# A token's gate matrix from a float32 product of 128 columns instead of a float32r product of 256

## The chip, the cores and the metric

The kernel runs on one core of a Trainium2 chip. The metric is the device time of one execution in microseconds (us), the median of several runs. In the rows, PE is TensorE (matrix products), PEld its loading of the stationary operand, DVE is VectorE, ACT is ScalarE, POOL is GpSimd and SP issues most loads.

## The reference, cut to what matters

One decoder layer over 512 tokens of width 2048: two token mixers, an output projection, a PEER channel mixer, a gated per-layer embedding and a last RMSNorm. The change lies in PEER. For each token, 8 heads choose 16 of 16384 experts each; an expert has the index `i1 * 128 + i2`, and a gate comes with it:

```python
e_idx = (jnp.take_along_axis(i1, ci // K, axis=-1) * PEER_NKEYS
         + jnp.take_along_axis(i2, ci % K, axis=-1))
gate = jax.nn.softmax(cv, axis=-1)
...
z = jnp.einsum('thkd,td->thk', u_tab[eb], hb)
a = jax.nn.gelu(z, approximate=False) * gb
return jnp.einsum('thk,thkd->td', a, v_tab[eb])
```

So a token has 128 pairs of an expert and a gate.

## The kernel before, in words

160 of the tokens go another way: their expert rows are gathered from memory by POOL, one row of every table access at a time, and DVE multiplies them (`row_op`, L915 and L924). The other 352 tokens are computed densely against all 16384 experts. The dense part has two stages. In the **u stage** a loop `j` over 128 tiles loads 128 experts' rows (1 MB), splits each float32 value into a high part (ACT, L115, written as float32r) and a low part (DVE, L116), and makes 48 products of 352 columns (L151, L152, L153). ACT applies the GELU (L1153). In the v stage the result, times the gates, is multiplied with the second table.

For that, each of the 352 tokens needs a matrix G of 128 by 128: the gate of expert (i1, i2) at row i1, column i2, and zero elsewhere. `gate_tokens` makes it during the u stage, four tokens at a time (a **quad** below; 88 in all). It compares a row of the numbers 0 to 127 (`iota`) with the token's 128 values of i1, which lie down the partitions, and so has a one-hot matrix `ohl` (two ACT operations, L997 and L1003). The same with i2, times the gate, is `ohr` (one DVE operation, L998). The product of the two (L1008) adds up 128 one-hot outer products into G. The products are float32r, a 4-byte format to which the code rounds; so the gate is held as a high and a low part, `ohr` has 2 times 128 columns, and the two halves of the result are added behind it, ACT copying the first (L1013) and DVE adding the second (L1014). `slots` holds i1, i2 and the two parts of the gate, transposed. A finished block of 32 tokens is stored by a transfer that ACT issues (L1016).

Three other lines come up below: L413 and L707 are float32 products of 128 by 128 (four for each of 8 heads in the first mixer, and the scores of the top-k), and L215 is a DVE operation of one scalar on a float32 matrix of 128 columns.

The order is written by hand. Each `j` takes steps of `gate_tokens` and of the top-k from a list by weights that the code states, and a fixed number of `row_op`; `gate_tokens` puts the quad's products behind that `j`'s 48 products, and its evacuation behind those of the next.

Of the kernel before, what the change touches and what calls it, by code (L numbers as in the profile page):

```python
# [10 lines left out]
F32 = mybir.dt.float32  # L11
F32R = mybir.dt.float32r
U32 = mybir.dt.uint32
I32 = mybir.dt.int32
AF = mybir.ActivationFunctionType
OP = mybir.AluOpType
# [34 lines left out]
def kernel(ctx: ExitStack, tc: tile.TileContext, a, dbg=None):  # L51
    nc = tc.nc
    dbg = dbg or {}
    V, S, G, TE = nc.vector, nc.scalar, nc.gpsimd, nc.tensor

    def flat(t):
        return t.rearrange("p a b -> p (a b)")
# [9 lines left out]
    def acc():  # L67
        return psA.tile([128, 512], F32, name="acc")
# [3 lines left out]
    def mx():  # L72
        return wide()[:, :512] if psW else psB.tile([128, 512], F32, name="mx")

    def wide():
        return psW.tile([128, 1024], F32, name="wide")

    def t2(name="t2", bufs=6):
        return tmp.tile([128, 512], F32, name="t2", bufs=bufs)
# [17 lines left out]
    class Stream:  # L97
# [14 lines left out]
        def split(self):  # L112
            for raw in self.raw:
                hi, lo = his(), los()
                S.activation(hi, raw, AF.Copy)  # L115
                V.tensor_tensor(lo, raw, hi.bitcast(F32), op=OP.subtract)  # L116
                self.parts.append((hi, lo))
# [46 lines left out]
    def cols_proj(src, xh, xl, kt=KT):  # L164

        w = Stream(src)
        ps = acc()
        for k in range(kt):
            mm3(ps, *w.part(k, kt), xh[:, k], xl[:, k], k == 0, k == kt - 1)
        return ps  # L170
# [74 lines left out]
    negmask, ident, iota = cst[:, :128], cst[:, 128:256], cst[:, 256:384]  # L245
# [5 lines left out]
    ones = const.tile([128, 128], F32, name="ones")  # L251
# [71 lines left out]
    for i in range(2):  # L323
        t = hg.tile([128, 4, 128], F32, name=f"abuf{i}")
# [10 lines left out]
    for hh in range(2):  # L335
# [25 lines left out]
        for c in range(4):  # L361
            ps = cols_proj(a["w_q"][hh * 4 + c], xh, xl)
            V.tensor_tensor(qT[:, c], ps, rr_mix, op=OP.mult)
        for c in range(4):
            ps = cols_proj(a["w_og"][hh * 4 + c], xh, xl)
# [24 lines left out]
        for h in range(4):  # L390
# [6 lines left out]
            for bb in range(2):  # L397
# [4 lines left out]
                o = slice(bb * 2, bb * 2 + 2)  # L402
# [15 lines left out]
            for n in range(7):  # L418
                dS = mx()
                r = slice((n % 2) * 64, (n % 2) * 64 + 64)  # L420
                TE.matmul(dS[:, :128], lhsT=k_t[r, n // 2, hs], rhs=v_t[r, n // 2, hs],
                          start=True, stop=True)
                st = hg.tile([128, 128], F32, name="st", bufs=8)
                if n == 0:
                    S.activation(st, dS[:, :128], AF.Copy)
                else:
                    V.scalar_tensor_tensor(st, states[-1], eb[:, n * 64 + 63:n * 64 + 64], dS[:, :128],
                                           op0=OP.mult, op1=OP.add)
                states.append(st)
            o_ps = mx()  # L430
            for b in range(4):
# [3 lines left out]
                for n in (2 * b, 2 * b + 1):  # L435
                    if n:
                        ns = slice(n * 64, n * 64 + 64)
                        TE.matmul(o_ps[:, ns], lhsT=states[n], rhs=qe[:, ns], start=False,
                                  stop=n == 2 * b + 1, skip_group_check=True)
# [28 lines left out]
    for name, src, gain in (("q", "w_mq", g_q), ("kv", "w_mkv", g_kv)):  # L468
# [3 lines left out]
        for c in range(4):  # L472
            ps = cols_proj(a[src][c], xh, xl)
            t = t2()
# [32 lines left out]
    ps = cols_proj(a["w_kr"][0], xh, xl)  # L507
    t = t2()
# [24 lines left out]
    for hp in range(4):  # L533
# [13 lines left out]
        for c in range(2):  # L547
            t = t2()
            V.tensor_tensor(t, lat_cols(c, qh, ql), rr_q, op=OP.mult)
            split(*qn[c], t)  # L550
        r, t = t2(), t2()
# [10 lines left out]
        for c in range(2):  # L562
            t = t2()
            V.tensor_tensor(t, lat_cols(c, vh, vl), rr_kv, op=OP.mult)
            split(*kn[c], t)
        for b, (bh, bl) in enumerate(vblocks):
            ps = acc()
            for k in range(4):
                hi, lo = w.part(k, 4)
# [6 lines left out]
        for c in range(2):  # L576
# [3 lines left out]
            for qb in range(4):  # L580
                n = (qb + 1) * 128
# [9 lines left out]
                st = tmp.tile([128, 4], F32, name="sm", bufs=4)  # L591
                V.tensor_reduce(st[:, 0:1], s_ps[:, :n], axis=AX.X, op=OP.max)
                V.tensor_scalar(st[:, 1:2], st[:, 0:1], -1.0, None, op0=OP.mult)
                p = t2()
# [9 lines left out]
                for kb in range(qb + 1):  # L604
                    TE.matmul(ob_ps[:, qs], lhsT=vv[:, kb, c * 128:c * 128 + 128],
                              rhs=pT[:, kb * 128:kb * 128 + 128], start=kb == 0, stop=kb == qb)
            t = t2()
# [135 lines left out]
    kpool = tc.alloc_tile_pool(name="kpool", bufs=1, side="left")  # L743
# [184 lines left out]
    def two(name, n=2):  # L928
        return (kpool.tile([128, 128], F32, name=name + str(i), bufs=2) for i in range(n))
# [13 lines left out]
    slots = {}  # L943
# [11 lines left out]
    def prep_B(b):  # L955
        i1, i2 = two("i")
        gt = kpool.tile([128, 128], F32, name="gt", bufs=1)

        def experts_X():
            e, x = t2()[:, :128], slice(0, NX)  # L960
            V.scalar_tensor_tensor(e[x], i1[x], 128.0, i2[x], op0=OP.mult, op1=OP.add)
            for r in range(RX):
                V.tensor_copy(eX[r * NX:(r + 1) * NX], e[x, r * NX:(r + 1) * NX])
                S.activation(gateX[r * NX:(r + 1) * NX], gt[x, r * NX:(r + 1) * NX], AF.Copy)

        def turn():
            slots[b] = kpool.tile([128, 4, 128], F32, name="slots", bufs=1)

            def pe():
                ps = mx()  # L970
                for n, t in enumerate((i1, i2, gt)):
                    TE.transpose(ps[:, n * 128:n * 128 + 128], t, ident)

                def act():
                    S.activation(flat(slots[b][:, :2]), ps[:, :256], AF.Copy)
                    split(slots[b][:, 2].bitcast(F32R), slots[b][:, 3], ps[:, 256:384])
                return act

            after_pe.append(lambda: after_pe_next.append(pe))
            hold[0] = 2  # L980

        return topk(b, i1, i2, gt) + ([(2, experts_X)] if b == 1 else []) + [(0, turn)]
# [3 lines left out]
    def gate_tokens(t0):  # L986

        if t0 % TC == 0:
            stage[0] = upool.tile([128, 128, TC], F32, name="stage", bufs=1)
        st = stage[0]  # L990
        hot = []
        for i in range(4):
            b, t = divmod(NA + NX + t0 + i, 128)
            l = upool.tile([128, 128], F32R, name="ohl", bufs=8)
            r = upool.tile([128, 2, 128], F32R, name="ohr", bufs=8)
            i1T, i2T = (slots[b][:, n, t:t + 1] for n in range(2))
            S.activation(l, iota, AF.Abs, scale=-1.0, bias=i1T)  # L997
            V.scalar_tensor_tensor(r, iota[:, None, :].to_broadcast([128, 2, 128]), i2T,  # L998
                                   slots[b][:, 2:4, t:t + 1].to_broadcast([128, 2, 128]),
                                   op0=OP.is_equal, op1=OP.mult)  # L1000
            hot.append((l, r))
        for l, _ in hot:
            S.activation(l, l.bitcast(F32), AF.Relu, scale=-1.0, bias=ones[:, :1])  # L1003

        def pe():
            ps = wide()
            for i, (l, r) in enumerate(hot):
                TE.matmul(ps[:, i * 256:i * 256 + 256], lhsT=l, rhs=flat(r), start=True, stop=True)  # L1008

            def act():  # L1010
                o = t0 % TC
                hi, lo = (ps.rearrange("p (t s j) -> p s j t", t=4, s=2)[:, n] for n in range(2))
                S.activation(st[:, :, o:o + 4], hi, AF.Copy)  # L1013
                V.tensor_tensor(st[:, :, o:o + 4], st[:, :, o:o + 4], lo, op=OP.add)  # L1014
                if o == TC - 4:
                    nc.scalar.dma_start(G_s[t0 // TC], flat(st))  # L1016
            return act

        after_pe.append(pe)
        if t0 % TC == TC - 4:  # L1020
            hold[0] = 2

    def merge(*lists):
# [3 lines left out]

    first = NA + NX
    quads = {b: [(2, lambda t=t - first: gate_tokens(t)) for t in range(max(b * 128, first), (b + 1) * 128, 4)]
             for b in (1, 2, 3)}  # L1030

# [33 lines left out]
    for n, (src, dst) in enumerate((("w_ga", ga_s[1]), ("w_gb", gb_s[1]))):  # L1065
        for i in range(16):
            w = block(a[src][i])
            ps = acc()[:, :H]
# [29 lines left out]
    for k in range(2):  # L1098
        r = t2()
# [4 lines left out]
    for m in range(16):  # L1104
# [5 lines left out]
        t = t2()  # L1110
# [30 lines left out]
    upool = tc.alloc_tile_pool(name="upool", bufs=1, side="left")  # L1141
# [37 lines left out]
    in_u, start = ops[0] - VROWS, ops[0]  # L1179
    for j in range(NU):  # L1180
# [5 lines left out]
        n = j + 1  # L1186
# [52 lines left out]
    def v_products(cur, grp, half):  # L1239
        ps = acc()[:, :ND]  # L1240
        for j in range(NJ):
            mm3(ps, *cur.part(half * NJ + j, 2 * NJ), *aT[grp, j], j == 0, j == NJ - 1)
        return ps

    NV = (NGRP - 1) * 8
    for grp in range(NGRP - 1):
        for dp in range(8):
            n = grp * 8 + dp
# [11 lines left out]
            for half in range(2):  # L1260
                ps = v_products(cur, grp, half)
# [33 lines left out]
    for dp in range(8):  # L1295
        cur = ahead.step()
        run_late()
        ps = [v_products(cur, NGRP - 1, half) for half in range(2)]
# [30 lines left out]
    for mt in range(16):  # L1329
# [8 lines left out]
        ps = acc()  # L1338
# [179 lines left out]
```

## Time and profile before

| | |
|---|---|
| median of three runs | 3962.06 us (3954.68 to 3966.48) |
| the profiled execution | 3957.45 us |
| its span in the trace | 3955.7 us |
| mean granted clock of TensorE in it | 0.993 of full |

The profiled execution's own time is its span and 1.75 us around it. The quads lie between 1754 us and 2676 us of that span.

### The profile page before, as it was taken

What the parts mean: (1) busy time and instruction counts of PE and PEld (TensorE: products, weight loads), DVE (VectorE), ACT (ScalarE), POOL (GpSimd) and SP (SyncE); (2) the same over time, 40 slices, a digit from 0 to 9 for tenths busy, and PEclk for the clock granted to TensorE, in tenths of its full rate; (3) what the DMA queues carried; (4) which work ended last, traced back from release to release, by engine and by line L of the source; (5) the groups of instructions that cost most, each with busy time, mean ns of one, the idle gap of its engine ahead of it and who ended that gap; (6) DMA issues with size and microseconds to landing.
All of it is one profiled execution on the core that took longest, in us unless ns stands there. A gap on an engine that the chain in (4) does not pass through costs nothing. (4 is left out here: it accounts for less than half of the span.)

```text
span 3955.7 us, 63576 instructions
## 1 busy us (share of the span) xinstructions
PE 3873.2 (98%) x24825; PEld 3677.9 (93%) x24825; DVE 2950.8 (75%) x4439; ACT 1750.3 (44%) x2814; POOL 496.4 (13%) x326
## 2 busy tenths in 40 slices
PE   9999999999999999899999999999999999999998
PEld 7878788899999989899999999999999999999987
DVE  5252555557658798789989898886888989899854
ACT  5242434345544434455555466663333333333443
POOL 0000000000000111012222222221122222222000
PEclk9999999999999999999999999999999999999999
DMA  5222234457766988788888888989999999899533
GB/s 212 96 75 96 70 99 134 130 184 238 231 203 205 330 280 299 268 293 314 317 319 301 306 324 308 338 310 357 359 346 346 368 356 353 330 360 361 195 120 99
DMA packets 312875, 1011.64 MB, mean 256 GB/s; under 512 B 29952, under 2 KB 127744, under 8 KB 269696
## 3 DMA queue, kind: packets, MB, share of 16 engines
q1 hardware_dynamic: 224032, 595.02, 44.1%
q0 software_dynamic: 46080, 335.56, 22.3%
q10 hardware_dynamic: 42464, 77.00, 5.1%
q8 instruction: 196, 3.21, 0.3%
q14 instruction: 103, 0.84, 0.1%
HBM read 931.18 MB, written 76.28 MB: 255 GB/s over the span
## 5 line engine op out<-in xcount | busy, mean ns | idle before, releaser
L116 DVE TENSOR_TENSOR lo<-raw,hi 128x1024 fp32r<-128x1024 f32 x966 | 1163.7, 1221 | 599.2 <-ACT hi L115 590.7
L115 ACT ACTIVATE hi<-raw 128x1024 fp32r<-128x1024 f32 x966 | 1012.5, 1056 | 1222.1 <-PE acc L152 819.1
L153 PE MATMUL acc<-hBh,lo 128*128 128x352 f32 x2048 | 662.1, 323 | 0.0
L152 PE MATMUL acc<-hBl,hi 128*128 128x352 f32 x2048 | 661.0, 323 | 0.0
L151 PE MATMUL acc<-hBh,hi 128*128 128x352 f32 x2048 | 658.7, 322 | 0.0
L904 POOL DMA_INDIRECT row<-in_peer_u_dram,eA x128 | 206.5, 1613 | 2194.2 <-PE acc L153 1298.8
L153 PEld LDWEIGHTS acc<-hBh,lo 128*128 128x128 f32 x2048 | 385.5, 188 | 0.0
L151 PEld LDWEIGHTS acc<-hBh,hi 128*128 128x128 f32 x2048 | 385.3, 188 | 0.0
L152 PEld LDWEIGHTS acc<-hBl,hi 128*128 128x128 f32 x2048 | 384.9, 188 | 0.0
L153 PE MATMUL acc<-ahx,lo 128*128 128x352 f32 x1024 | 331.5, 324 | 2.0 <-DVE lo L116 1.9
L151 PE MATMUL acc<-ahx,hi 128*128 128x352 f32 x1024 | 329.9, 322 | 1.1 <-DVE x L1237 1.1
L153 PE MATMUL acc<-ah,lo 128*128 128x352 f32 x1024 | 330.4, 323 | 0.5 <-DVE lo L116 0.5
L151 PE MATMUL acc<-ah,hi 128*128 128x352 f32 x1024 | 330.9, 323 | 0.0
L152 PE MATMUL acc<-alx,hi 128*128 128x352 f32 x1024 | 330.4, 323 | 0.0
L152 PE MATMUL acc<-al,hi 128*128 128x352 f32 x1024 | 329.0, 321 | 0.0
L151 PE MATMUL acc<-xh,hi 128*128 128x256 f32 (+1 forms) x912 | 305.1, 335 | 0.0
L153 PE MATMUL acc<-xh,lo 128*128 128x256 f32 (+1 forms) x912 | 305.0, 334 | 0.0
L152 PE MATMUL acc<-xl,hi 128*128 128x256 f32 (+1 forms) x912 | 304.2, 334 | 0.0
L924 DVE SCALAR_TENSOR_TENSOR hrow<-row,zA,hrow 128x2048 f32<-128x2048 f32 x127 | 297.9, 2345 | 0.8
L915 DVE SCALAR_TENSOR_TENSOR row<-row,hrow 128x2048 f32<-128x2048 f32 x128 | 291.6, 2281 | 6.8 <-DMA row<-in_peer_u_dram,eA 6.8
L904 POOL DMA_INDIRECT row<-in_peer_v_dram,eA x128 | 188.2, 1470 | 645.3 <-DVE hrow L924 610.5
L153 PEld LDWEIGHTS acc<-ahx,lo 128*128 128x128 f32 x1024 | 192.6, 188 | 3.7 <-DVE lo L116 3.7
(434 smaller groups left out, 8430.7 us busy)
## 6 DMA issues: line engine op xcount, KB each, us to landing
raw<-in_uT_dram SPq DMA_DIRECT2D x256, 512.0 KB, 7.5
raw<-in_vB_dram SPq DMA_DIRECT2D x256, 512.0 KB, 8.4
raw<-in_w_ga_dram SPq DMA_DIRECT2D x64, 512.0 KB, 4.2
raw<-in_w_gb_dram SPq DMA_DIRECT2D x64, 512.0 KB, 4.7
raw<-in_w_o_dram SPq DMA_DIRECT2D x64, 512.0 KB, 4.9
raw<-in_wq_dram SPq DMA_DIRECT2D x64, 512.0 KB, 4.7
z_s<-t ACTq DMA_DIRECT2D x128, 176.0 KB, 6.7
G_s<-stage ACTq DMA_DIRECT2D x11, 2048.0 KB, 15.0
```

What stands on the lines that cost most here:

```text
L115: S.activation(hi, raw, AF.Copy)
L116: V.tensor_tensor(lo, raw, hi.bitcast(F32), op=OP.subtract)
L151: TE.matmul(out, lhsT=lh, rhs=rh, start=start, stop=False)
L152: TE.matmul(out, lhsT=lh, rhs=rl, start=False, stop=False)
L153: TE.matmul(out, lhsT=ll, rhs=rh, start=False, stop=stop)
L904: G.indirect_dma_start(out=row, out_offset=None, in_=a["peer_v" if v else "peer_u"], in_offset=bass.IndirectOffsetOnAxis(ap=e[:, s:s + 1], ...
L915: V.scalar_tensor_tensor(row, row, 1.0, hrowX if x else hrow, op0=OP.mult, op1=OP.mult, accum_out=(zX if x else zA)[:, s:s + 1])
L924: V.scalar_tensor_tensor(o, row, c[:, s:s + 1], o, op0=OP.mult, op1=OP.add)
```

## The change: what it does

The quad's products become float32 products of 128 columns: `ohl` and `ohr` are float32, `ohr` holds the whole gate in one 128 by 128 matrix, and the result needs no addition, so ACT's copy alone takes it into `stage`. `slots` holds three transposed blocks instead of four, and one ACT copy fills it.

```diff
@@ turn, in prep_B @@
-            slots[b] = kpool.tile([128, 4, 128], F32, name="slots", bufs=1)
+            slots[b] = kpool.tile([128, 3, 128], F32, name="slots", bufs=1)
...
-                    S.activation(flat(slots[b][:, :2]), ps[:, :256], AF.Copy)
-                    split(slots[b][:, 2].bitcast(F32R), slots[b][:, 3], ps[:, 256:384])
+                    S.activation(flat(slots[b]), ps[:, :384], AF.Copy)
@@ gate_tokens @@
-            l = upool.tile([128, 128], F32R, name="ohl", bufs=8)
-            r = upool.tile([128, 2, 128], F32R, name="ohr", bufs=8)
-            i1T, i2T = (slots[b][:, n, t:t + 1] for n in range(2))
+            l = upool.tile([128, 128], F32, name="ohl", bufs=8)
+            r = upool.tile([128, 128], F32, name="ohr", bufs=8)
+            i1T, i2T, gT = (slots[b][:, n, t:t + 1] for n in range(3))
             S.activation(l, iota, AF.Abs, scale=-1.0, bias=i1T)
-            V.scalar_tensor_tensor(r, iota[:, None, :].to_broadcast([128, 2, 128]), i2T,
-                                   slots[b][:, 2:4, t:t + 1].to_broadcast([128, 2, 128]),
-                                   op0=OP.is_equal, op1=OP.mult)
+            V.tensor_scalar(r, iota, i2T, gT, op0=OP.is_equal, op1=OP.mult)
...
-            S.activation(l, l.bitcast(F32), AF.Relu, scale=-1.0, bias=ones[:, :1])
+            S.activation(l, l, AF.Relu, scale=-1.0, bias=ones[:, :1])
...
-            ps = wide()
+            ps = mx()
             for i, (l, r) in enumerate(hot):
-                TE.matmul(ps[:, i * 256:i * 256 + 256], lhsT=l, rhs=flat(r), start=True, stop=True)
+                TE.matmul(ps[:, i * 128:i * 128 + 128], lhsT=l, rhs=r, start=True, stop=True)
...
-                hi, lo = (ps.rearrange("p (t s j) -> p s j t", t=4, s=2)[:, n] for n in range(2))
-                S.activation(st[:, :, o:o + 4], hi, AF.Copy)
-                V.tensor_tensor(st[:, :, o:o + 4], st[:, :, o:o + 4], lo, op=OP.add)
+                S.activation(st[:, :, o:o + 4], ps.rearrange("p (t j) -> p j t", t=4), AF.Copy)
```

The order of the instructions stays: on every engine each remaining instruction stands between the same neighbours as before, and rows are replaced or left out. On PE, at the first two quads of the u stage, the products of a whole `j` stand ahead (`hBh`, `hBl`, `hi` and `lo` are the operands of L151 to L153); before:

```order
L152 MATMUL acc<-hBl,hi_77 128x352
L153 MATMUL acc<-hBh,lo_81 128x352
L1008 MATMUL wide<-ohr,ohl 128x256 x8
L151 MATMUL acc<-hBh,hi_78 128x352
L152 MATMUL acc<-hBl,hi_78 128x352
```

and with the change:

```order
L152 MATMUL acc<-hBl,hi_77 128x352
L153 MATMUL acc<-hBh,lo_81 128x352
L1005 MATMUL wide<-ohr,ohl 128x128 x8
L151 MATMUL acc<-hBh,hi_78 128x352
L152 MATMUL acc<-hBl,hi_78 128x352
```

The quad's products keep their place; the line is now L1005. On DVE, from the same two quads on (`row` and `zA` are `row_op`'s, `scores` and `val` the top-k's), before:

```order
L998 SCALAR_TENSOR_TENSOR ohr<-cst,slots 128x256 x8
L915 SCALAR_TENSOR_TENSOR row_6472,zA<-row_6472,hrow 128x2048
L116 TENSOR_TENSOR lo_80<-raw_72,hi_76 128x1024
L116 TENSOR_TENSOR lo_81<-raw_73,hi_77 128x1024
L1014 TENSOR_TENSOR stage<-stage,wide 128x128x4 x2
L830 MAX val<-scores 128x8 x2
```

and with the change:

```order
L997 TENSOR_SCALAR ohr<-cst,slots 128x128 x8
L915 SCALAR_TENSOR_TENSOR row_6472,zA<-row_6472,hrow 128x2048
L116 TENSOR_TENSOR lo_80<-raw_72,hi_76 128x1024
L116 TENSOR_TENSOR lo_81<-raw_73,hi_77 128x1024
L830 MAX val<-scores 128x8 x2
```

The addition is gone and the one-hot operation is another one of half the columns; nothing else on DVE changes its place.

## Rows read from the trace of the kernel before

**Rows 1.** The page's first part: each engine's busy time over the span.

```profile
PE 3873.2 (98%) x24825; PEld 3677.9 (93%) x24825; DVE 2950.8 (75%) x4439; ACT 1750.3 (44%) x2814; POOL 496.4 (13%) x326
```

**Rows 2.** Windows of the u stage: the stretch, its length, busy us of each engine.

```profile
1734.00:2690.00 956.00, 951.39 (x5990) 946.22 (x5989) 855.76 (x1391) 552.04 (x1159) 217.16 (x126) 1.00 0.87 316
...
2500.00:2600.00 100.00, 100.00 (x640) 100.00 (x640) 87.62 (x115) 65.88 (x147) 23.82 (x14) 1.00 0.89 323
```

**Rows 3.** The quads' products, line L1008: counts, durations, idle time before them.

```profile
L1008 PEld LDWEIGHTS wide<-ohr,ohl x352: 186/188/288, 1756.9 to 2672.3; 128*128 128x128 f32 x176
L1008 PE MATMUL wide<-ohr,ohl x352: 274/281/554, 1757.1 to 2672.4; 128*128 128x256 f32 x176
its engine sat idle before it (us, times) until:
  issue: 4.3, 17
  DVE ohr L998: 3.1, 3
  ACT t L1153: 2.8, 2
  ACT ohl L1003: 2.1, 3
  ACT hi L115: 0.2, 1
  ACT stage L1013: 0.2, 1
```

**Rows 4.** Timeline of PE at the first two quads: start us, length us.

```profile
1757.05 1.10 PE L1008 MATMUL wide<-ohr,ohl 128*128 128x256 f32 x8
1757.99 0.32 PE L151 MATMUL acc<-hBh,hi 128*128 128x352 f32 x1
1758.15 0.32 PE L152 MATMUL acc<-hBl,hi 128*128 128x352 f32 x1
```

**Rows 5.** Timeline of PE at two float32 products of 128 columns, L707.

```profile
1733.39 0.33 PE L153 MATMUL acc<-hBh,lo 128*128 128x352 f32 x1
1733.56 0.61 PE L707 MATMUL mx<-kk_t,t 128*128 128x128 f32 x4
1733.92 0.41 PE L151 MATMUL acc<-hBh,hi 128*128 128x352 f32 x1
1734.16 0.32 PE L152 MATMUL acc<-hBl,hi 128*128 128x352 f32 x1
```

**Rows 6.** Timelines of PE at four float32 products in a row, L413, twice.

```profile
200.47 1.05 PE L413 MATMUL mx<-e,e 128*128 128x128 f32 x8
201.45 0.71 PE L421 MATMUL mx<-v_t,k_t 64*128 64x128 f32 x6
...
227.60 1.16 PE L413 MATMUL mx<-e,e 128*128 128x128 f32 x8
228.69 0.71 PE L421 MATMUL mx<-v_t,k_t 64*128 64x128 f32 x6
```

**Rows 7.** Line L413 over the whole span: counts, durations ns.

```profile
L413 PEld LDWEIGHTS mx<-e,e x64: 186/192/193, 200.3 to 449.1; 128*128 128x128 f32 x64
L413 PE MATMUL mx<-e,e x64: 270/275/374, 200.5 to 449.2; 128*128 128x128 f32 x64
```

**Rows 8.** Timeline of DVE and PE around the latest quads.

```profile
2068.71 3.26 DVE L998 SCALAR_TENSOR_TENSOR ohr<-cst,slots 128x256 fp32r<-128x256 f32 x8
2076.37 1.27 DVE L1014 TENSOR_TENSOR stage<-stage,wide 128x512 f32<-128x512 f32 x2
2079.92 1.66 DVE L998 SCALAR_TENSOR_TENSOR ohr<-cst,slots 128x256 fp32r<-128x256 f32 x4
2084.45 1.74 PE L1008 MATMUL wide<-ohr,ohl 128*128 128x256 f32 x4 [2.38 <-DVE ohr L998]
```

**Rows 9.** Timeline of DVE at four float32 TENSOR_SCALAR of 128 columns, L215.

```profile
3772.73 0.87 DVE L215 TENSOR_SCALAR t<-cst,rc_ple 128x128 f32<-128x128 f32 x4
```

## The prediction

> **What bounds the kernel now.** I read the page's busy shares first [rows 1]: PE is busy for 3873.2 of 3955.7 us, and the next engine, DVE, for 75%. A share over the whole span says little about one stage, so the windows of the u stage come next, in which all 88 quads lie [rows 2]. From 1734 to 2690 us PE is busy for 951.4 of 956.0 us, DVE for 855.8. PE waits for almost nothing there, and where no quad is late (2500 to 2600 us, 13 quads) for nothing at all. So whatever is put on PE in this stage comes out at the end, and what is taken from DVE or ACT counts only as far as PE waits for it.
>
> Then the changed line itself [rows 3]. It has one record for each of its 352 products, and the idle times ahead of it add up to 4.3 + 3.1 + 2.8 + 2.1 + 0.2 + 0.2 = 12.7 us. That is an upper bound on what less work on DVE and ACT can give back here; some of it counts one wait twice, for the load and for the product behind it, and the idle time of PE in rows 2 is only 4.6 us.
>
> Last, the price of a product. A record's duration (281 ns at the median) is no price, since products overlap. The price is the distance from one start to the next, so I read timelines.
>
> **What PE pays.** Before: eight products of two quads start at 1757.05, and the next L151 at 1757.99 [rows 4]. That is 0.94 us, 0.1175 us for a product, 0.47 us for a quad, and 352 x 0.1175 = 41.4 us in all.
>
> After: the trace has no float32 product with these operands, but float32 products of 128 rows by 128 columns elsewhere. The nearest are the two of L707 that stand, as the quads will, between products of 352 columns [rows 5]. They leave four records, two for each product. From their start at 1733.56 to the second product behind them, at 1734.16, it is 0.60 us; one product of 352 columns takes 0.16 us of it (from L151 to L152 in rows 4). The L151 between is drawn early and long, so its own start is no good mark. That leaves 0.44 us for two, 0.22 us for one, 0.88 us for a quad. In all 352 x 0.22 = 77.4 us.
>
> The difference is 77.4 - 41.4 = **+36.0 us**, 0.41 us for a quad.
>
> The other rows give the bounds. L413 has four float32 products in a row, each with its own stationary operand, as a quad has. Eight records take 0.98 us to the next start, and 1.09 us in another place [rows 6]: 0.245 and 0.273 us a product, +44.8 and +54.7 us in all. No row is below 0.22 us. I take 0.22, because rows 5 has the quads' neighbours, while in rows 6 the next product has 64 rows and may itself start late, and because a quad's operands are ready long before its turn but for the waits counted below.
>
> A rule of the Trainium skill speaks against this change. Its page "TensorE: Matmul & The Clock Gate", section "Weight-path perf modes", says that the fast way to load the stationary operand is not used for FP32. The rows show no slower load: 192 ns at the median for L413's float32 operand [rows 7], 188 ns for float32r [rows 3]. What loads that could not be hidden would do is a rival below.
>
> **What the waits give back.** On DVE the four `ohr` operations of a quad halve their columns and become TENSOR_SCALAR. Eight of before take 3.26 us, 0.41 each [rows 8]; four float32 TENSOR_SCALAR of 128 columns take 0.87 us, 0.22 each [rows 9]. Those have one scalar operand from a column and the new one has two, as the old one has; I take 0.22, with 0.41 as the other end. The addition L1014 goes, 1.27 / 2 = 0.64 us. Together 4 x 0.19 + 0.64 = 1.4 us for a quad, 123 us of DVE. None of it is on PE's path except where PE waits for `ohr`.
>
> The largest such wait is 2.38 us at 2084.45 [rows 8]. Ahead of it DVE does twelve `ohr` operations and two additions from 2068.71 on, with other work between; with the change that is 12 x 0.19 + 1.27 = 3.6 us less, more than the wait. So waits of this kind go. What stays is what ACT ends: its two operations for `ohl` keep their number and size, and PE waits 2.1 us for them [rows 3]. I take **-10 us** of the 12.7; the ends are 0 and -12.7.
>
> **The rest at nothing.** One ACT copy instead of the three operations for `slots` happens three times in the run, beside PE's 48 x 0.16 = 7.7 us of products in a `j`. ACT's copy into `stage` has the same 512 columns. The result's buffer holds 512 columns instead of 1024 but comes from the same two, in the same turn. No transfer, no gather and no `row_op` moves, since their number in each `j` is fixed, so the v stage begins later by what the u stage takes longer, and no queue is passed. If the new `ohr` cost as much as the old, those 7.7 us would still hide it as they do now, and only the waits would not go: +36.
>
> **Sum.** 36.0 - 10 = +26.0 us on an execution of 3957.45 us (span 3955.7 and 1.75 around it): 3983.5 us. The median of the runs shown is 3962.06, 4.6 us above that execution, so in such a median I expect **3988 us**.
>
> **Rivals.**
>
> *The second pass starts late in each quad.* The 1.09 us of rows 6 would be the rule, not the exception: 54.7 - 10 = +44.7, 4007 us. For it speaks that PE comes to a quad with other operands than those of its 48 products; against it rows 5, with the same neighbours. Chance 0.14. I count in it the case that the waits stay (+36 to +45).
>
> *Loads bind.* Eight loads of 192 ns [rows 7], if they did not lie beside the passes, take 1.54 us a quad instead of 0.47: +94, less 10, 4046 us. Against it: rows 6 has eight records with eight loads in 0.98 us. Chance 0.03. The Trainium skill's page "FP8 and Floating Point Precision", section "TensorE Precision Notes", gives a true FP32 product four passes through the array. The rows show two records a product, so by the rule each record would stand for two passes; four passes at a record's 0.11 us would be +113 us, and rows 5 and 6 exclude that.
>
> *One pass (the other side).* If the new product went through once, as the old does, half the columns would take half the time: 0.059 us, 0.235 us a quad, -20.7 us, and with the waits -31 us, 3931 us. It decides where a quad costs less than 0.47 + 10 / 88 = 0.58 us. Against it: 64 records for L413's 32 products [rows 7] (four for each of 8 heads), and four for two in rows 5. Chance 0.03.
>
> *It cancels.* Two passes of 0.059 us, half a record's 0.11 us, would be 0.1175 us a product, as before, and only the waits would count: -10 us, 3952 us, which is within 0.3%. Against it rows 5 again. Chance 0.05, with all else that ends near zero, such as waits outside rows 3 that go with DVE's 123 us.
>
> That the change would not do what it says I leave at nothing: the built order has the new rows in the old places.
>
> **How the numbers follow.** Forecast 0.75, late second pass 0.14, loads 0.03, one pass 0.03, cancels 0.05. A measurement of this kernel can tell about 0.3% (12 us) from no change, so slower is 0.75 + 0.14 + 0.03 = 0.92, same 0.05, faster 0.03. The range's low end is the forecast with all 12.7 us back, 3985, less 6 us for half the spread of the three runs: 3979. Its high end is the price of rows 6 with no wait gone, +45, 4007, and with it the first rival's 4007: I take 4008.
>
> **What would show it.** In the changed kernel's profile L1005 should have 704 product records and 704 loads, and two quads should keep PE for about 1.76 us to the next L151 or L152 instead of 0.94; a quad at 1.0 or more is the first rival, and 352 records the third. DVE's busy time over the u stage should fall by about 120 us, and PE should still be busy for over 99% of it. The idle times ahead of the quads' products should add up to 3 us or so. The u stage should end some 26 us later, and every stage outside it should take what it takes now. The prediction is wrong if a float32 pass costs something else between these neighbours than between L707's, or if PE waits for DVE somewhere that I have not seen.

## The result: 26 us slower

The changed kernel takes 3986.5 us in the median of five runs (3985.12 to 3995.72), beside 3960.49 us (3954.68 to 3966.48) for five runs of the kernel before. The ratio of the mean times is 1.0072, with a 95% interval from 1.0055 to 1.0088, that is 22 to 35 us. The forecast was 3988 us, 26 us more. That the two medians differ by just these 26.0 us is luck: such runs can't tell it so closely.

The page of the changed kernel, first part, answers to [rows 1]:

```profile
PE 3904.4 (98%) x25177; PEld 3713.3 (93%) x25177; DVE 2851.5 (72%) x4348; ACT 1754.5 (44%) x2811; POOL 465.4 (12%) x326
```

PE has 25177 products instead of 24825, so 352 more, one for each token. DVE does 99 us less work. The stage in which the quads lie, by the first and the last start of L151's products in the u stage (its row by line, before and then the changed kernel):

```profile
L151 PE MATMUL acc<-hBh,hi x2048: 317/323/496, 1725.8 to 2764.2; 128*128 128x352 f32 x187
```

```profile
L151 PE MATMUL acc<-hBh,hi x2048: 318/324/408, 1727.5 to 2791.6; 128*128 128x352 f32 x187
```

The stage takes 1038.4 us before and 1064.1 after: 25.7 us more. The two profiled executions differ by 28.7 us of span (3984.4 and 3955.7 us), and the other 3.0 us lie ahead of the u stage (1.7 us) and behind it. Below, "the u stage" is this length, read in the same way from each run's trace.

The windows of the u stage, drawn 26 us longer, and the changed line, answer to [rows 2] and [rows 3]:

```profile
1734.00:2716.00 982.00, 980.95 (x6345) 980.75 (x6344) 756.74 (x1303) 555.35 (x1156) 187.26 (x127) 1.00 0.85 309
```

```profile
L1005 PEld LDWEIGHTS wide<-ohr,ohl x704: 186/192/192, 1758.6 to 2699.7; 128*128 128x128 f32 x176
L1005 PE MATMUL wide<-ohr,ohl x704: 270/275/348, 1758.8 to 2699.8; 128*128 128x128 f32 x176
...
its engine sat idle before it (us, times) until:
  ACT hi L115: 1.2, 1
  DVE ohr L997: 1.1, 1
```

Each product has two records and two loads. PE is busy for 99.9% of the stage, and the idle times ahead of the quads are 2.3 us instead of 12.7 (here one wait of 1.1 us, counted for the load and again for the product). The first two quads in the timeline of PE, which answer to [rows 4]:

```profile
1758.79 1.95 PE L1005 MATMUL wide<-ohr,ohl 128*128 128x128 f32 x16
1760.49 0.41 PE L151 MATMUL acc<-hBh,hi 128*128 128x352 f32 x1
1760.74 0.32 PE L152 MATMUL acc<-hBl,hi 128*128 128x352 f32 x1
```

From 1758.79 to the second product behind, 1760.74, less 0.16 us for one product of 352 columns, is 1.79 us for eight products: 0.224 us each. In the whole trace 75 of the 76 places where quads stand (12 of them hold two) cost 0.112 us a record in this way; in the other one PE waits for `ohr`.

### The profile page after: what moved, and what is told of

Its sections match the earlier page's. It is cut to its first block, busy times and chain, and to the rows that moved or that the text cites. A ratio compares the mean times of both kernels' runs of the same rounds, so it can differ in the third digit from the quotient of the medians.

```text
span 3984.4 us, 64143 instructions
## 1 busy us (share of the span) xinstructions
PE 3904.4 (98%) x25177; PEld 3713.3 (93%) x25177; DVE 2851.5 (72%) x4348; ACT 1754.5 (44%) x2811; POOL 465.4 (12%) x326
## 3 DMA queue, kind: packets, MB, share of 16 engines
q8 instruction: 199, 3.26, 0.3%
## 5 line engine op out<-in xcount | busy, mean ns | idle before, releaser
L151 PE MATMUL acc<-hBh,hi 128*128 128x352 f32 x2048 | 664.3, 324 | 0.0
L153 PE MATMUL acc<-hBh,lo 128*128 128x352 f32 x2048 | 661.3, 323 | 0.0
L152 PE MATMUL acc<-hBl,hi 128*128 128x352 f32 x2048 | 660.5, 323 | 0.0
L904 POOL DMA_INDIRECT row<-in_peer_u_dram,eA x128 | 196.7, 1537 | 2217.2 <-PE acc L153 1299.2
L151 PEld LDWEIGHTS acc<-hBh,hi 128*128 128x128 f32 x2048 | 384.9, 188 | 0.0
L153 PEld LDWEIGHTS acc<-hBh,lo 128*128 128x128 f32 x2048 | 384.9, 188 | 0.0
L152 PEld LDWEIGHTS acc<-hBl,hi 128*128 128x128 f32 x2048 | 384.8, 188 | 0.0
L153 PE MATMUL acc<-ahx,lo 128*128 128x352 f32 x1024 | 331.3, 324 | 2.8 <-DVE lo L116 2.7
L151 PE MATMUL acc<-ahx,hi 128*128 128x352 f32 x1024 | 329.7, 322 | 2.1 <-DVE x L1232 2.1
L151 PE MATMUL acc<-ah,hi 128*128 128x352 f32 x1024 | 330.5, 323 | 0.2 <-DVE x L1232 0.2
L152 PE MATMUL acc<-alx,hi 128*128 128x352 f32 x1024 | 330.3, 323 | 0.0
L153 PE MATMUL acc<-ah,lo 128*128 128x352 f32 x1024 | 329.6, 322 | 0.5 <-DVE lo L116 0.5
L152 PE MATMUL acc<-al,hi 128*128 128x352 f32 x1024 | 328.6, 321 | 0.0
L151 PE MATMUL acc<-xh,hi 128*128 128x256 f32 (+1 forms) x912 | 304.9, 334 | 0.0
L153 PE MATMUL acc<-xh,lo 128*128 128x256 f32 (+1 forms) x912 | 304.8, 334 | 0.0
L152 PE MATMUL acc<-xl,hi 128*128 128x256 f32 (+1 forms) x912 | 304.0, 333 | 0.0
L153 PEld LDWEIGHTS acc<-ahx,lo 128*128 128x128 f32 x1024 | 192.5, 188 | 4.8 <-DVE lo L116 4.8
```

The lines of the kernel that those rows point to most:

```text
L151: TE.matmul(out, lhsT=lh, rhs=rh, start=start, stop=False)
L152: TE.matmul(out, lhsT=lh, rhs=rl, start=False, stop=False)
L153: TE.matmul(out, lhsT=ll, rhs=rh, start=False, stop=stop)
L904: G.indirect_dma_start(out=row, out_offset=None, in_=a["peer_v" if v else "peer_u"], in_offset=bass.IndirectOffsetOnAxis(ap=e[:, s:s + 1], ...
```

## The experiments

The first question was what sets a product's price: the columns that are streamed, or something that comes once a record, such as the load. The second was who gave back the waits. In the diffs, `...` stands for lines left out.

**1. float32r, 128 columns, one pass.** Against the changed kernel:

```diff
-            l = upool.tile([128, 128], F32, name="ohl", bufs=8)
-            r = upool.tile([128, 128], F32, name="ohr", bufs=8)
+            l = upool.tile([128, 128], F32R, name="ohl", bufs=8)
+            r = upool.tile([128, 128], F32R, name="ohr", bufs=8)
...
```

> The changed kernel with float32r operands instead of float32: one pass of 128 columns, and the gate rounded once, its low part left out. DVE's work is that of the changed kernel. Theory (a pass takes as long as its columns stream): half of the 0.1175 us of 256 columns, 0.059 us a product, 0.235 us a quad, so PE saves 88 x 0.235 = 20.7 us against before and the waits give back 11.6 us more (13.1 us of excess in the u stage before, 1.5 with the change): about 3928 us. Rival (a pass can't be shorter than the loading of its stationary operand lets it, about 0.11 us): 0.112 us a product, 0.45 us a quad, 3960.5 - 2 - 11.6 = 3947 us.

Measured 3951.57 us beside 3963.93 for the kernel before, ratio 0.9971 (0.9960 to 0.9983). Its timeline of PE at one quad:

```profile
1777.55 0.56 PE L1005 MATMUL wide<-ohr,ohl 128*128 128x128 f32 x4
1777.94 0.38 PE L151 MATMUL acc<-hBh,hi 128*128 128x352 f32 x1
1778.15 0.33 PE L152 MATMUL acc<-hBl,hi 128*128 128x352 f32 x1
```

Four products take 1778.15 - 1777.55 - 0.16 = 0.44 us, 0.11 each. Half the columns cost what 256 columns do, 0.1175. My theory fell, and the rival holds: something other than the columns sets the price.

**2. float32, 64 columns.** Against the changed kernel:

```diff
-                TE.matmul(ps[:, i * 128:i * 128 + 128], lhsT=l, rhs=r, start=True, stop=True)
+                TE.matmul(ps[:, i * 64:i * 64 + 64], lhsT=l, rhs=r[:, :64], start=True, stop=True)
...
```

> The changed kernel with 64 columns a product instead of 128, still float32; the columns 64 to 127 of each gate matrix are left out and filled with the first 64. Loads are as many and as large as with the change, the streamed columns are half. Theory (columns decide): 0.056 us a pass, 0.45 us a quad instead of 0.89, so 39 us less than with the change: 3947 us. Rival (loads decide): 0.112 us a pass, 0.89 us a quad, the time of the changed kernel, 3986 us.

Measured 3991.74 us, ratio 1.0073 (1.0059 to 1.0088), as the changed kernel. The u stage is 1064.3 us, as the changed kernel's 1064.1. One quad:

```profile
1774.17 1.00 PE L1005 MATMUL wide<-ohr,ohl 128*128 128x64 f32 x8
1774.98 0.41 PE L151 MATMUL acc<-hBh,hi 128*128 128x352 f32 x1
1775.22 0.32 PE L152 MATMUL acc<-hBl,hi 128*128 128x352 f32 x1
```

1775.22 - 1774.17 - 0.16 = 0.89 us for eight records, 0.11 each: the rival again. With one pass or two, with 64, 128 or 256 columns, a record takes 0.11 to 0.12 us. What is alike in all of them is a load of 128 by 128 four-byte values.

**3. Is it the load? 64 columns of the stationary operand.** Against the changed kernel, with the float32r operands of experiment 1:

```diff
...
-                TE.matmul(ps[:, i * 128:i * 128 + 128], lhsT=l, rhs=r, start=True, stop=True)
+                TE.matmul(ps[:64, i * 128:i * 128 + 128], lhsT=l[:, :64], rhs=r, start=True, stop=True)
...
```

> The first experiment (float32r, 128 columns, 0.112 us a product, 3951.6 us) with 64 columns of the stationary operand instead of 128: rows 64 to 127 of each gate matrix are left out and filled with the first 64, which costs ACT a second copy for each quad. The streamed columns stay at 128. Theory (what keeps a product of few columns from taking less than 0.112 us is the loading of its stationary operand): half the load, 0.056 to 0.06 us a product, 88 x 4 x 0.053 = 19 us less than the first experiment, 3933 us. Rival (a product has a fixed least time whatever it loads): 0.112 us a product, 3951 us.

Measured 3944.19 us beside 3961.1, ratio 0.9960 (0.9945 to 0.9976). The time fell by less than expected. The price inside a quad fell as the theory says, the price of a whole quad not quite as far:

```profile
1772.27 0.40 PE L1005 MATMUL wide<-ohr,ohl 128*64 128x128 f32 x4
1772.51 0.38 PE L151 MATMUL acc<-hBh,hi 128*128 128x352 f32 x1
1772.72 0.32 PE L152 MATMUL acc<-hBl,hi 128*128 128x352 f32 x1
```

1772.72 - 1772.27 - 0.16 = 0.29 us. Within the quad the starts are 0.06 us apart: the four records span 0.40 us, the last one's own duration (223 ns at the median) taken off and the rest divided by three. That is half of experiment 1's price, and the load's record is shorter too, 135 ns at the median instead of 190. The whole quad costs 0.29 us and not 4 x 0.06 = 0.24. Three steps of 0.06 and one of 0.11 us make 0.29, as if the first load behind the quad, which again has 128 columns of four bytes, showed in full; no run tests this apart. So PE's price fell by 88 x (0.44 - 0.29) = 13 us of the 19. The u stage fell by 4.8 us, to 1023.9, and the other 8 went into waits, in the row of the line:

```profile
its engine sat idle before it (us, times) until:
  ACT ohl L1000: 14.0, 24
```

PE now waits for `ohl` from ACT (the 14.0 us count some waits twice, for the load and for the product). ACT has a second copy for each quad here, which is the likely reason, not tested apart. The edit also halves the rows of the result; the next experiment has all 128 of them.

**4. The same columns, another type: bfloat16.** Against the changed kernel:

```diff
-            l = upool.tile([128, 128], F32, name="ohl", bufs=8)
-            r = upool.tile([128, 128], F32, name="ohr", bufs=8)
+            l = upool.tile([128, 128], BF16, name="ohl", bufs=8)
+            r = upool.tile([128, 128], BF16, name="ohr", bufs=8)
```

> The first experiment with bfloat16 operands instead of float32r: 128 columns, one pass, the gate rounded to bfloat16 and the rest of it left out (the one-hot operand is exact). As many columns and as many rows of the stationary operand; only the type of the load differs. Theory (the loading of a 128-column float32 or float32r operand, 186 ns a record and 0.112 us from one to the next, is what held the first experiment; a bfloat16 load is shorter): 0.056 us a product, 0.22 us a quad, 88 x 0.22 = 20 us less than the first experiment, about 3932 us (the first was 0.9971 of before). Rival (a load takes the same for every type): 0.112 us a product, 3951 us.

Measured 3946.89 us beside 3964.89, ratio 0.9958 (0.9943 to 0.9973). The line's rows:

```profile
L1006 PEld LDWEIGHTS <-ohl x352: 94/98/105, 1762.6 to 2658.9; 128*128 128x128 bf16 x176
L1006 PE MATMUL wide<-ohr,ohl x352: 216/219/266, 1762.6 to 2658.9; 128*128 128x128 bf16 x176
...
  ACT ohl L1001: 6.6, 11
  DVE ohr L998: 3.8, 2
```

and one quad in the timeline of PE (this kernel has one line more at its head, so L152 here is L151 of the others):

```profile
1778.52 0.40 PE L1006 MATMUL wide<-ohr,ohl 128*128 128x128 bf16 x4
1778.73 0.41 PE L152 MATMUL acc<-hBh,hi 128*128 128x352 f32 x1
1778.97 0.32 PE L153 MATMUL acc<-hBl,hi 128*128 128x352 f32 x1
```

The load's record is 98 ns instead of 186 to 192, and a quad takes 1778.97 - 1778.52 - 0.16 = 0.29 us, with (0.40 - 0.22) / 3 = 0.06 us from one start in it to the next. The u stage is 1019.3 us, 9.4 below experiment 1's 1028.7. Of the 20 us that were expected, 13 are in the price (0.29 us a quad instead of the expected 0.22), and 4 of these went into waits. The theory of the load holds: with full columns and all rows of the result the step is again 0.06. The type of the streamed operand changed as well, but in experiment 3 that stayed at four bytes and the step fell all the same.

**5 and 6. Two products of 128 columns into the same PSUM, float32r and bfloat16.** PSUM is where the products are written and, here, added up. The kernel before, with this edit and without the addition on DVE; experiment 6 has bfloat16 operands besides:

```diff
-                TE.matmul(ps[:, i * 256:i * 256 + 256], lhsT=l, rhs=flat(r), start=True, stop=True)
+                for n in range(2):
+                    TE.matmul(ps[:, i * 128:i * 128 + 128], lhsT=l, rhs=r[:, n], start=n == 0, stop=n == 1)
...
```

> The kernel before, but the high and the low half of the gate go through two float32r products of 128 columns that add into the same 128 columns of PSUM, so that the addition on DVE goes. The output is exact as before. As many streamed columns as before, twice the loads, as with the change. Theory (loads decide): 8 products of 0.112 us, 0.89 us a quad, the price of the change, +37 us, and with only the addition off DVE some 5 to 10 us of waits back: 3988 to 3996 us. Rival (columns decide): 0.47 us a quad as before, 3953 to 3958 us.

> The fifth experiment with bfloat16 operands: the gate as a high and a low bfloat16 part (16 bits of it are kept, the rest is left out), two products of 128 columns a token that add into the same PSUM columns, no addition on DVE. Eight products and eight loads a quad as in the changed kernel and the fifth experiment. Theory (short loads): 8 x 0.056 = 0.45 us a quad, PE as before, and with the addition off DVE about 5 us of waits back: 3955 us, 30 us below the fifth experiment. Rival (a load takes the same for every type): as the fifth experiment, 3988 us.

The float32r version takes 3987.94 us beside 3961.1, ratio 1.0074 (1.0059 to 1.0090); the bfloat16 version 3957.63 beside 3964.89, ratio 0.9988 (0.9979 to 0.9997). Their timelines at one quad, float32r and then bfloat16:

```profile
1771.90 1.00 PE L1009 MATMUL wide<-ohr,ohl 128*128 128x128 f32 x8
1772.74 0.38 PE L151 MATMUL acc<-hBh,hi 128*128 128x352 f32 x1
1772.95 0.33 PE L152 MATMUL acc<-hBl,hi 128*128 128x352 f32 x1
```

```profile
1777.65 0.62 PE L1013 MATMUL wide<-ohr,ohl 128*128 128x128 bf16 x8
1778.09 0.41 PE L152 MATMUL acc<-hBh,hi 128*128 128x352 f32 x1
1778.33 0.32 PE L153 MATMUL acc<-hBl,hi 128*128 128x352 f32 x1
```

0.89 us against 0.52, with the same eight products of 128 columns. Both came out as the theory of the load expected. So the changed kernel's price can be had without float32: eight loads of four-byte operands a quad, where the kernel before has four.

**7. DVE's saving alone.** PE's products are those of before (float32r, 256 columns), DVE's work is that of the change. Against the changed kernel:

```diff
...
-                TE.matmul(ps[:, i * 128:i * 128 + 128], lhsT=l, rhs=r, start=True, stop=True)
+                TE.matmul(ps[:, i * 256:i * 256 + 256], lhsT=l, rhs=r[:, None, :].to_broadcast([128, 2, 128]),
+                          start=True, stop=True)
...
```

> PE's work of before (float32r, 256 columns a product) with DVE's work of the change: one TENSOR_SCALAR of 128 columns for each token, which the product streams twice, and no addition; the low part of the gate is left out. Theory (what DVE saves gives back PE's waits in the u stage and nothing else): 0.1175 us a product as before, 11 to 12 us less than before, 3949 us. Rival (the waits went because PE got slower, not because DVE got faster): as before, 3960 us.

Measured 3951.8 us beside 3963.93, ratio 0.9972 (0.9960 to 0.9984), so 6 to 16 us less, as the theory says. The u stage is 1030.7 us, 7.7 below before. The latest quad still waits, in the timeline of PE:

```profile
2081.96 0.86 PE L1005 MATMUL wide<-ohr,ohl 128*128 128x256 f32 x4
2085.05 1.32 PE L1005 MATMUL wide<-ohr,ohl 128*128 128x256 f32 x4 [2.23 <-DVE ohr L997]
```

Ahead of that wait DVE does its work sooner than before and then stands idle itself. Its timeline between the quads before the change, and here:

```profile
2074.10 2.35 DVE L116 TENSOR_TENSOR lo<-raw,hi 128x1024 fp32r<-128x1024 f32 x2
2077.57 0.48 DVE L830 MAX8 val<-scores 128x8 f32<-128x128 f32 x2
```

```profile
2074.98 2.36 DVE L116 TENSOR_TENSOR lo<-raw,hi 128x1024 fp32r<-128x1024 f32 x2 [1.43 <-ACT hi L115]
2078.85 0.49 DVE L830 MAX8 val<-scores 128x8 f32<-128x128 f32 x2 [1.51 <-DMA scores<-sc]
```

DVE waits 1.43 us for ACT and 1.51 us for the transfer of the top-k's scores, and these 2.9 us are about what it had saved up to there: 3.26 - 2.14 = 1.1 us on eight `ohr` operations, 1.27 on the two additions and 0.29 on `slots`.

**8. PE's price alone.** PE's products are those of the change, DVE's work is that of before. Against the changed kernel:

```diff
-            r = upool.tile([128, 128], F32, name="ohr", bufs=8)
+            r = upool.tile([128, 2, 128], F32, name="ohr", bufs=8)
...
+                V.tensor_tensor(st[:, :, o:o + 4], st[:, :, o:o + 4], g4, op=OP.max)
...
```

> PE's work of the change (float32, 128 columns) with DVE's work of before: the one-hot operation on 256 columns, of which the product takes the first 128, and an operation on the evacuated result and its PSUM copy that is as long as the addition was and leaves the values as they are. Theory (DVE's saving gives back about 11.6 us): the price of 37 us with most of the waits back, 3960.5 + 37 = 3997 us, less up to 5 us since PE's longer quads give DVE 0.42 us each: 3992 to 3997 us. Rival (the slower PE alone takes the waits away): as the changed kernel, 3986 us.

Measured 3990.53 us beside 3963.93, ratio 1.0067 (1.0055 to 1.0079). By the times alone it can't be told from the changed kernel, and it lies below the theory's range (3992 to 3997 us beside 3960.5). The kept trace is of the slowest of the six runs, 4001.21 us. In it the u stage is 1070.0 us, 5.9 longer than the changed kernel's, and the large wait is there:

```profile
2096.40 1.05 PE L1008 MATMUL wide<-ohr,ohl 128*128 128x128 f32 x8
2099.71 2.05 PE L1008 MATMUL wide<-ohr,ohl 128*128 128x128 f32 x8 [2.26 <-DVE ohr L998]
```

To read 7 and 8 together, take the price of the quads off each u stage, so that waits and all else remain. The price is 41.4 us for float32r of 256 columns and 352 x 0.224 = 78.8 us for float32:

| | u stage | price | remains |
|---|---|---|---|
| before | 1038.4 | 41.4 | 997.0 |
| light DVE, PE of before (7) | 1030.7 | 41.4 | 989.3 |
| DVE of before, slow PE (8) | 1070.0 | 78.8 | 991.2 |
| the change | 1064.1 | 78.8 | 985.3 |

Of the 11.7 us that the change gets back, DVE's saving alone gives 7.7 and the longer quads alone 5.8. Each theory had half of it, and the two nearly add up.

The whole times (7 and 8) are too coarse for this and speak for 11 us in either case, so it rests on single traces. Counted at the quads alone (from the start of the product ahead of them to the second product behind, less 0.32 us and the price), the time over the price is 12.5 us before, 4.9 in 7, 6.7 in 8 and 1.3 with the change. All the rest of the stage is 984 to 985 us in these four, so the halves aren't an accident of it.

**9. The kernel before once more.**

> The kernel before once more, for a second trace. Theory (the waits ahead of the quads are the same in each execution, since the order is fixed): 12 to 14 us of excess over the price of the products in the u stage, with the large wait at the same quad. Rival (they depend on when transfers land): an excess that differs by several us.

The u stage is 1040.0 us, 998.6 of them beside the quads' price. At the quads alone the time over the price is 12.8 us, as expected (12.5 in the first trace), and the large wait is at the same quad, in the timeline of PE:

```profile
2084.07 1.74 PE L1008 MATMUL wide<-ohr,ohl 128*128 128x256 f32 x4 [2.37 <-DVE ohr L998]
2085.61 0.50 PE L151 MATMUL acc<-hBh,hi 128*128 128x352 f32 x1
2085.90 0.49 PE L152 MATMUL acc<-hBl,hi 128*128 128x352 f32 x1
```

So the waits belong to the order, as far as two traces show, and differences of 6 to 8 us between u stages stand against 1.6 us between two traces of one kernel.

These rows show something that the count of waits leaves out. Behind the large wait two products of 352 columns start 0.29 us apart instead of 0.16. Windows of 1 us at the same quad in the first trace of the kernel before, during the wait and behind it, and then in the changed kernel's (the third figure from the end is the granted clock as a share of the full 2.4 GHz):

```profile
2083.00:2084.00 1.00, 0.00 (x0) 0.00 (x0) 1.00 (x8) 0.68 (x2) 0.00 (x0) 1.00 0.04 16
2087.00:2088.00 1.00, 1.00 (x5) 1.00 (x4) 1.00 (x3) 1.00 (x5) 0.03 (x1) 0.50 0.00 0
```

```profile
2091.00:2092.00 1.00, 0.20 (x2) 0.23 (x2) 1.00 (x6) 1.00 (x2) 0.00 (x0) 1.00 0.10 41
2092.00:2093.00 1.00, 1.00 (x9) 1.00 (x9) 1.00 (x3) 0.60 (x2) 0.00 (x0) 1.00 0.00 0
```

Behind the wait of 2.38 us the clock was at its lower level, 1.2 GHz, until 2088 us; behind the change's wait of 1.05 us it stayed at the full one. It fell in 7 and 8 too, behind 2.23 and 2.26 us. In the first trace 7 products of 352 columns run at the lower level, in this second one 17; at some 0.14 us each that is an estimated 1 and 2 us, and most of the 1.6 us between the two traces. So the shorter wait also spared PE a stretch at the lower level, which the prediction has nowhere.

**10. The low half of `ohr` on POOL.** This keeps the kernel before's products and all of its gate.

```diff
-            V.scalar_tensor_tensor(r, iota[:, None, :].to_broadcast([128, 2, 128]), i2T,
-                                   slots[b][:, 2:4, t:t + 1].to_broadcast([128, 2, 128]),
-                                   op0=OP.is_equal, op1=OP.mult)
+            for n, E in enumerate((V, G)):
+                E.tensor_scalar(r[:, n], iota, i2T, slots[b][:, 2 + n, t:t + 1], op0=OP.is_equal, op1=OP.mult)
```

> The kernel before, exact, with the high half of the one-hot operand as a TENSOR_SCALAR of 128 columns on DVE and the low half as the same on POOL. PE's work is that of before. Theory (0.76 us a quad off DVE, about half of what the change takes off it, gives back about half of what the second experiment gave): 5 to 6 us less than before in the u stage. Rival (POOL's operation takes over a microsecond, or it and DVE slow each other, and the quads or the gathers come late): as before or slower.

(The second experiment of that text is number 7 here.)

Measured 4048.24 us beside 3961.1, ratio 1.0222 (1.0208 to 1.0236). The line's rows:

```profile
L999 POOL TENSOR_SCALAR ohr<-cst,slots x352: 780/834/5798, 1746.4 to 2750.1; 128x128 fp32r<-128x128 f32 x176
L999 DVE TENSOR_SCALAR ohr<-cst,slots x352: 323/343/702, 1750.5 to 2750.3; 128x128 fp32r<-128x128 f32 x176
...
who waited for it (us, times):
  PEld wide L1007: 62.4, 55
  PE wide L1007: 48.3, 45
```

POOL takes 834 ns at the median and up to 5798 for what DVE does in 343, and PE waits for it (the two rows count a wait for the load and again for the product): the rival holds. Why single operations on POOL take so long, no run shows.

## Why the prediction was right, step by step

**PE is the bound of the u stage.** Right: PE is busy for 980.95 of 982 us, and of the 99 us that DVE saves over the span the end sees only waits.

**What PE pays.** Forecast 0.22 us a product and +36.0 us; measured 0.224 us, 352 x 0.224 - 41.4 = +37.4 us. The choice of [rows 5] over [rows 6] was the right one: the neighbours decide. Within the eight records of [rows 6] the steps are 0.11 us as well; the trace before has the rest at their edges, 0.205 us from the last record to L421 and, in the second place, 0.21 us in the first step, where the load had waited for `e` from DVE. A late second pass is in no quad of the changed kernel's trace.

**What a product's price is made of.** Here the prediction was wrong in its reasons. It read the equal load records, 192 and 188 ns, as a sign that loads don't matter. They do: both kinds are slow, and it is the load that holds a record at 0.112 us (experiments 1 to 6). The old product hid its one load behind 256 columns (256 x 0.16 / 352 = 0.116 us); the new one has two loads with 128 columns each, and they show. The rule of the Trainium skill that was set aside there, that FP32 operands get no fast load (its page "TensorE: Matmul & The Clock Gate", section "Weight-path perf modes"), bears on this. The traces agree with it: float32's load records are 192 ns at the median, bfloat16's 98. That float32r's are as long as float32's, 188 to 190 ns, is why the comparison in the prediction showed nothing. That the loads bind was a rival with a chance of 0.03, priced at +94 us, since I took loads as standing in a row at their records' length. They overlap, and in the changed kernel's trace one starts every 0.112 us. The number came out right all the same because the rows of L707, from which the price was read, hold the same loads.

**One pass.** The rival's price of 0.059 us was wrong as well: experiment 1 is that case, and takes 0.11.

**What the waits give back.** Forecast -10 us; measured 12.7 - 2.3 = 10.4 us of idle time ahead of the quads, and 11.7 us by the table above. The size was right, the cause was half of it: I gave all to DVE. The largest wait falls by little with DVE's saving alone (2.38 to 2.23 us) and with the slow PE alone (2.26), and to 1.1 us with both. The step that failed is the one from 3.6 us less work ahead of that wait to no wait: DVE's own waits for ACT and for the scores took up what it saved (7). Nor did the waits stay that I expected to stay: the row of L1005 has none for `ohl`, and the one that is left is for `ohr`. The lower clock behind the large wait was in no term (9). Forecast and measurement agree so well in part because the forecast's price was 1.4 us too low and its give-back 1.7 us too low, and the two cancel.

DVE's saving was put at 1.4 us a quad, 123 us. By the two lines it is 108 us, mostly because the new operation takes 2.14 us for eight, 0.27 each, and not 0.22; over the span it is 99 us, as other records of DVE came out a little longer. That is hidden.

**The rest at nothing.** Right: the stage ahead of the u stage and those behind it differ by 3.0 us between two executions.

## What to carry to other kernels

A small product on TensorE pays for its load: ask how many loads of four-byte operands an edit adds before asking how many columns it streams, and remember that with such operands a record of 128 columns and one of 256 cost nearly the same here. When work is to come off a busy vector engine, first see in the stage's windows and in the waits of the bound engine how much of it can come back; here 99 us of DVE were worth some 8 us of the u stage (experiment 7). Then follow the saved time along that engine's own order: at its next wait for another engine or a transfer the saving can be gone. If the low bits of a one-hot product's factor can be spared, one pass is a little faster than both kernels (experiment 1: 0.9971 of before, the gate rounded once); with two short loads of bfloat16, 16 bits of it can be kept at 0.9988.

## What the runs showed of the hardware that I had not expected

- A record with a 128 by 128 stationary operand takes 0.11 us in float32 with 64 or 128 streamed columns and in float32r with 128, and 0.1175 in float32r with 256. With 64 columns of the stationary operand in float32r, or with bfloat16 operands, one step within a quad is 0.06 us, though a whole quad of four costs 0.29.
- A float32 product of 64 columns and one of 128 take the same 0.22 us.
- POOL's TENSOR_SCALAR on 128 by 128 takes 0.83 us at the median and 1.33 on average, DVE's 0.34.
- Behind a wait of 2.2 to 2.4 us TensorE's granted clock fell to 0.50 in three kernels (before, 7 and 8), and products of 352 columns then stood 0.29 to 0.30 us apart instead of 0.16; behind one of 1.05 us it stayed at 1.00.
